# Strassen products of a feed-forward block in float32: copies that free PSUM banks put right behind their products, weight sums one split ahead, another order of small products

## The chip, the core and the metric

The kernel runs on one core of a Trainium2 chip. Its time is the device time of one execution in microseconds (us); the time before is the median of three runs. The engines are TensorE (PE, matrix products; PEld is its weight load), VectorE (DVE), ScalarE (ACT), GpSimd (POOL) and SyncE (SP), which here only issues DMAs. Each engine works through its own queue in order.

## The reference, cut to what matters

One step of a two-layer encoder for a prompt of 1024 frames and a sample of 32: in the first layer an mLSTM mixer, in the second a windowed attention, each followed by a SwiGLU feed-forward block. The change touches the feed-forward block alone:

```python
def swiglu(x, w_gu, w_down):
    g, u = jnp.split(x @ w_gu, 2, axis=-1)
    return (jax.nn.silu(g) * u) @ w_down
...
x = layer_norm(DEEPNORM_ALPHA * x + swiglu(x, w_gu[layer], w_down[layer]), ln_g[layer, 1], ln_b[layer, 1])
```

The model width is 1024, the inner width 2816, everything is float32.

## The kernel before, in words

**Float32 by three products.** Each operand is split into a high part (rounded to the PE's fp32r type) and the remainder. `gemm` (L404) issues three matmuls per tile of 128 rows: high by high (L412), high by low (L413), low by high (L414). Weights are split on the fly: ACT makes `wh` (L244), then POOL, for some units DVE, makes `wl` (L246).

**Seven products for eight.** The 1056 frames are four groups of 264 columns. In the feed-forward block a weight is halved both ways, a1, a2, b1, b2, and multiplied by Strassen's seven products in Winograd's form: a1, a2, b2 and the sums s1 to s4, with the operands x11, x21, x22 and t1 to t4 of the activations. Four DVE operations make the sums of a pair of raw weight tiles in place (L212 to L218). The inner width is 22 tiles of 128; tiles 2, 3, 20 and 21 of a layer are worked by `up_tile`, tiles 4 to 19 in eight *doubles* by `up_double(i)` (L1565), which takes tiles i and i + 1 as rows 0 and 1 and applies the seven-product scheme a second time to the products by a2: four small weights g1 to g4 (from the tile `wn`, with sums at L194 to L197) make seven small products into the PSUM tiles `chain` and `side`.

A large product is 24 matmuls of 264 columns, a small one 6. A double has 12 large and 7 small ones, 330 matmuls. `chain` accumulates, as bank A does: a1's product, then s2, s1 and s4 are added on top without clearing, and after each of the first three ACT copies the sum so far out of A (to gate0 at L1607, to up0 at L1618, to up1 at L1624); after s4 ACT applies SiLU (L1635). So the next product into A must wait for the copy. b2 and s3 go to bank B, of which a double has one; DVE adds them (L1621, L1627, L1628).

In a row the order of products is a1, the pair of small ones, s2, b2, s1, s3, (row 1: the pair for g3), s4 (row 1: g4).

**What sets the order of the other engines.** `Weights` keeps a list of split jobs. `_next` (L221) takes the next one: loads raw tiles if need be, makes the sums that this job needs on DVE (`_source`, L200, and `_inner`, L188), then issues ACT's copy and POOL's subtraction. `done` (L274) is called when a product has been issued and, with five slots, issues the split four jobs ahead. `mul` calls `done` at its end, and the copy out of A is issued after `mul`: behind that split in ACT's queue. The raw tiles (four buffers, `wr`) are loaded by `load_to` (L166) when a pair's last split, s4, has been issued, `wn` (one buffer) by `fetch` (L176) when g4's has.

**Staging.** `stage(p)` (L1375) is a task that runs beside the products: it takes finished inner tiles, makes t1 to t4 of them on DVE (L1398, L1399, L1404, L1411), splits each by `put` (ACT L1386, POOL or DVE L1387) and stores it (L1388, `hs`). It frees the buffer slots that later copies out of A write to. The down product reads the stores back.

## Time and profile before

| what | value |
|---|---|
| median of 3 runs | 2264.77 us (2258.8 to 2269.38) |
| the profiled execution | 2263.57 us, span 2261.8 us |
| mean granted PE clock | 0.994 |
| PE, PEld busy | 2185.3 us, 2147.7 us |
| DVE, ACT, POOL busy | 1567.8, 1015.0, 1077.7 us |
| the chain that ended last | PE 63%, DVE 15%, ACT 7% |

How to read the views: a group or timeline row names the line, the engine, the operation, what is written from what (128x512 is partitions by elements) and times. In a group row, behind the bar, stand busy time, mean ns of one, and the engine's idle time just before these instructions with what ended it. A timeline row has the start, the duration, and in brackets the idle time before it and the instruction that released it. A row of windows has the stretch, its length, then for PE, PEld, DVE, ACT and POOL busy time and count, the granted clock, the DMA engines' busy share and GB/s. A matmul's modelled duration is longer than the distance to the next one's start, because matmuls are pipelined.

### The profile page before, as it was taken

How to read it: one execution, taken by the hardware profiler on the slowest of the kernel's cores; microseconds unless marked ns; L12 is line 12 of the kernel's file. 1: busy time of each engine (PE TensorE's matmuls, PEld its weight loads, DVE VectorE, ACT ScalarE, POOL GpSimd, SP SyncE). 2: the span in 40 equal slices, each digit the busy share in tenths (PEclk: the TensorE clock that was granted, in tenths of full speed). 3: DMA queues.
4: the chain of work that ended last, by engine and by line, in shares of the span. 5: the costliest groups of instructions: out<-in, count | busy, mean ns of one | idle time of the engine just before them, and what ended most of it. 6: DMA issues, size and time to landing. Idle time of an engine off the chain costs nothing.

```text
span 2261.8 us, 44523 instructions
## 1 busy us (share of the span) xinstructions
PE 2185.3 (97%) x16990; PEld 2147.7 (95%) x16990; DVE 1567.8 (69%) x3008; ACT 1015.0 (45%) x2299; POOL 1077.7 (48%) x1014
## 2 busy tenths in 40 slices
PE   9999999999999999999999999999899999999997
PEld 9999999998899999999998999999899999999997
DVE  4465677787677776566667678888677777666657
ACT  4444455463444444422236778656344444431224
POOL 2544210004667667544526777501566766654431
PEclk9999999999999999999999999999999999999999
DMA  4222213113344444797515334412344344398622
GB/s 166 76 60 58 67 35 109 53 67 114 141 154 144 151 152 153 255 330 236 182 65 172 105 105 109 154 38 77 118 158 171 124 162 171 127 357 280 225 71 78
DMA packets 181414, 315.16 MB, mean 139 GB/s; under 512 B 18832, under 2 KB 131528, under 8 KB 181200
## 3 DMA queue, kind: packets, MB, share of 16 engines
q1 hardware_dynamic: 176848, 307.98, 41.2%
q10 hardware_dynamic: 4352, 4.33, 0.6%
q8 instruction: 134, 2.20, 0.4%
q14 instruction: 80, 0.66, 0.1%
HBM read 214.51 MB, written 87.27 MB: 133 GB/s over the span
## 4 chain that ended last, share of the span: by engine, by line
PE 63%; DVE 15%; ACT 7%; issue 6%; DMA 5%; POOL 4%; SPq 0%; POOLq 0%; ACTq 0%; DVEq 0%
PE d L412 9%; PE d L414 9%; PE d L413 9%; PE A L412 6%; PE A L414 6%; PE A L413 6%; PE B L412 4%; PE B L413 4%; PE B L414 4%; DMA wn<-in_gu 2%; DVE z L1599 1%; PE T L2021 1%; POOL wl_b L246 1%; DVE wr L218 1%; ACT act L515 1%
## 5 line engine op out<-in xcount | busy, mean ns | idle before, releaser
L246 POOL TENSOR_TENSOR wl_s<-wr,wh_s 128x512 fp32r<-128x512 f32 x224 | 329.1, 1488 | 203.6 <-ACT wh_s L244 152.2
L412 PE MATMUL d<-sx,wh 128*128 128x264 f32 (+2 forms) x1068 | 342.2, 320 | 2.5 <-ACT wh L244 2.4
L414 PE MATMUL d<-sx,wl 128*128 128x264 f32 (+2 forms) x1068 | 326.2, 305 | 2.7 <-POOL wl L246 2.7
L413 PE MATMUL d<-sx,wh 128*128 128x264 f32 (+2 forms) x1068 | 325.8, 305 | 0.2
L246 POOL TENSOR_TENSOR wl_a<-wr,wh_a 128x512 fp32r<-128x512 f32 x80 | 109.6, 1370 | 428.2 <-ACT wh_a L244 426.5
L412 PE MATMUL A<-sx,wh_s 128*128 128x264 f32 x896 | 259.2, 289 | 19.3 <-ACT z L1624 5.4
L244 ACT CAST wh_s<-wr 128x512 fp32r<-128x512 f32 x224 | 135.7, 618 | 284.6 <-DVE wr L216 256.6
L414 PE MATMUL A<-sx,wl_s 128*128 128x264 f32 x896 | 255.5, 285 | 0.0
L413 PE MATMUL A<-sx,wh_s 128*128 128x264 f32 x896 | 255.4, 285 | 0.0
L412 PEld LDWEIGHTS d<-sx,wh 128*128 128x128 f32 x1068 | 202.4, 189 | 6.1 <-ACT wh L244 3.1
L414 PEld LDWEIGHTS d<-sx,wl 128*128 128x128 f32 x1068 | 202.1, 189 | 3.9 <-POOL wl L246 3.6
L413 PEld LDWEIGHTS d<-sx,wh 128*128 128x128 f32 x1068 | 202.6, 190 | 1.6 <-DVE sx L443 0.8
L412 PEld LDWEIGHTS A<-sx,wh_s 128*128 128x128 f32 x896 | 169.9, 190 | 26.0 <-ACT z L1624 7.5
L412 PE MATMUL d<-sx,ex 128*128 128x264 f32 x624 | 180.5, 289 | 0.1
L413 PE MATMUL d<-sx,ex 128*128 128x264 f32 x624 | 177.2, 284 | 0.0
L414 PE MATMUL d<-sx,ex 128*128 128x264 f32 x624 | 176.9, 284 | 0.0
L414 PEld LDWEIGHTS A<-sx,wl_s 128*128 128x128 f32 x896 | 170.1, 190 | 0.0
L413 PEld LDWEIGHTS A<-sx,wh_s 128*128 128x128 f32 x896 | 170.0, 190 | 0.0
L412 PE MATMUL A<-ex,wh_s 128*128 128x264 f32 x448 | 130.1, 290 | 22.9 <-ACT z L1607 14.7
L246 POOL TENSOR_TENSOR wl<-wr,wh 128x512 fp32r<-128x512 f32 (+2 forms) x81 | 104.4, 1297 | 95.8 <-ACT wh L244 93.9
L2001 POOL TENSOR_SCALAR s<-s,st 128x256 f32<-128x256 f32 (+1 forms) x144 | 122.7, 864 | 44.6 <-DVE st L1999 29.9
L246 POOL TENSOR_TENSOR wl_g<-wn,wh_g 128x512 fp32r<-128x512 f32 x64 | 92.9, 1452 | 80.4 <-ACT wh_g L244 78.9
(438 smaller groups left out, 7464.6 us busy)
## 6 DMA issues: line engine op xcount, KB each, us to landing
wr<-in_gu SPq DMA_DIRECT2D x92, 512.0 KB, 5.1
hs_t<-act SPq DMA_DIRECT2D x64, 528.0 KB, 4.9
hs_x<-act SPq DMA_DIRECT2D x56, 528.0 KB, 2.9
sx<-hs_x SPq DMA_DIRECT2D x112, 264.0 KB, 6.0
sx<-hs_t SPq DMA_DIRECT2D x64, 264.0 KB, 6.0
ex<-hs_t SPq DMA_DIRECT2D x64, 264.0 KB, 6.3
wr<-in_dn SPq DMA_DIRECT2D x32, 512.0 KB
hs_x<-z SPq DMA_DIRECT2D x16, 528.0 KB, 6.2
```

The costliest lines, as they stand in the source:

```text
L218: sub(a2, a2, b2)
L244: self.nc.scalar.copy(hi, r)
L246: eng.tensor_sub(lo, r, hi.bitcast(F32))
L412: nc.tensor.matmul(out, ah, bh, start=start and k == 0, stop=False, **kw)
L413: nc.tensor.matmul(out, ah, bl, start=False, stop=False, **kw)
L414: nc.tensor.matmul(out, al, bh, start=False, stop=stop and k == last, **kw)
L515: nc.scalar.activation(z, z, AF.Identity, scale=gk, bias=bk)
L1599: nc.vector.tensor_mul(gate0[r], gate0[r], up0[r])
L2001: nc.gpsimd.tensor_scalar_mul(p[:R, h, lo:256], p[:R, h, lo:256], st[:R, 2, h : h + 1])
L2021: nc.tensor.transpose(pt[:nk, i, h, :R], p[:R, h, c : c + nk], ident[:R, :R])
```

## The change

It does five things: in `up_double`, the copies out of bank A (and the SiLU) are issued by a callback at the end of the product, before `done` issues the next split; the order of products in a row becomes a1, b2, s2, small pair, s1, s3 and the rest as before, with the job list to match; the four sums of a pair are formed in another order and in other places (s2 in a1's, s3 in b2's, s4 in a2's, s1 in b1's), and `prepare` issues those of the next job right behind the current split; loads of raw tiles and the fetch of `wn` are issued at the next job instead of at once; and the splits of the nested operands start 1.0 us later each.

```diff
-                self.jobs += [(u, f) for f in ("a1", "g1", "b2", "s2", "s1", "s3", "s4")]
-                self.jobs += [(v, "a1"), (u, "g2")] + [(v, f) for f in ("b2", "s2", "s1", "s3")]
-                self.jobs += [(u, "g3"), (v, "s4"), (u, "g4")]
+                self.jobs += [(u, f) for f in ("a1", "b2", "s2", "g1", "s1", "s3", "s4")]
+                self.jobs += [(v, f) for f in ("a1", "b2", "s2")] + [(u, "g2")]
+                self.jobs += [(v, f) for f in ("s1", "s3")] + [(u, "g3"), (v, "s4"), (u, "g4")]
...
-        if f == "g2":
-            s3, a1, a2, b1, b2 = (part(i) for i in range(5))
-            self.nc.vector.tensor_sub(s3, a1, b1)
-            self.nc.vector.tensor_add(b1, b1, b2)
-            self.nc.vector.tensor_sub(a1, b1, a1)
-            self.nc.vector.tensor_sub(a2, a2, a1)
...
+        self.prepare(u, f)
+        a, b = self.raw[u], self.raw[u + 1]
+        return {
+            "a1": a[:, :n], "a2": a[:, n : 2 * n], "b2": b[:, n : 2 * n],
+            "s1": b[:, :n], "s2": a[:, :n], "s3": b[:, n : 2 * n], "s4": a[:, n : 2 * n],
+        }[f]
+
+    def prepare(self, u, f):
+
+        if (u, f) in self.made or f not in ("s2", "s3", "s4", "g2"):
+            return
+        self.made.add((u, f))
         sub, add = self.nc.vector.tensor_sub, self.nc.vector.tensor_add
-        if f == "b2":
-
-            sub(a1, a1, b1)
-        elif f == "s2":
-
+        if f == "g2":
+            t = self.inner[u]
+            s3, a1, a2, b1, b2 = (t[:, 256 * i : 256 * (i + 1)] for i in range(5))
+            sub(s3, a1, b1)
+        else:
+            n = self.units[u].shape[-1] // 2
+            a, b = self.raw[u], self.raw[u + 1]
+            a1, a2, b1, b2 = a[:, :n], a[:, n : 2 * n], b[:, :n], b[:, n : 2 * n]
+        if f in ("s2", "g2"):
             add(b1, b1, b2)
+            sub(a1, b1, a1)
+        if f == "s3":
             sub(b2, b2, a1)
-        elif f == "s1":
-            sub(a2, a2, b2)
+        if f in ("s4", "g2"):
+            sub(a2, a2, a1)
...
+        self.load_to(self.due)
         self.load_to(u if f in (0, 1) else u + 1)
+        if self.owed:
+            self.owed = False
+            self.fetch()
...
         if f == "g4":
             del self.inner[u]
-            if self.nfetch % len(DOUBLES):
-                self.fetch()
-        if f in (1, "s4"):
+            self.owed = self.nfetch % len(DOUBLES) > 0
+        if f == 1:
             del self.raw[u]
-            if f == "s4":
-                del self.raw[u + 1]
-                u += 1
             self.load_to(u + self.depth)
+        if f == "s4":
+            del self.raw[u], self.raw[u + 1]
+            self.due = u + 1 + self.depth
+        if self.njob < len(self.jobs):
+            u, f = self.jobs[self.njob]
+            if u in self.inner if f == "g2" else u in self.raw and u + 1 in self.raw:
+                self.prepare(u, f)
...
                 hi, lo = nested[o]
-                yield 1.2
+                yield 2.2
...
-            def mul(row, ps, f, o, **kw):
+            def mul(row, ps, f, o, then=None, **kw):
...
+                if then:
+                    then()
                 W.done(us[row], f)
...
+            def copy_to(at, name, row, ps):
+                at[row] = take(row, name)
+                nc.scalar.copy(at[row], ps)
+
             for row in range(2):
                 a = bank("A")
-                mul(row, a, "a1", "x11")
-                gate0[row] = take(row, "g0")
-                nc.scalar.copy(gate0[row], a)
+                mul(row, a, "a1", "x11", lambda: copy_to(gate0, "g0", row, a))
                 finish_tile()
+                if not row:
+                    staging.append(wv.launch(stage(i // 2 - 1)))
+                b = bank("B")
+                mul(row, b, "b2", "t4")
+                mul(row, a, "s2", "t2", lambda: copy_to(up0, "u0", row, a), again=True)
+                nc.vector.tensor_add(up0[row], up0[row], b)
                 if row:
                     small(chain, "g2", 1, "t2", [(1, 0)], True, False)
                     small(side, "g2", 0, "t3", [(1, 1)])
                 else:
-                    staging.append(wv.launch(stage(i // 2 - 1)))
                     small(chain, "g1", 0, "x11", [(0, 0)], False, False)
                     small(side, "g1", 1, "x21", [(0, 0)])
-                mul(row, a, "s2", "t2", again=True)
-                up0[row] = take(row, "u0")
-                nc.scalar.copy(up0[row], a)
-                b = bank("B")
-                mul(row, b, "b2", "t4")
-                nc.vector.tensor_add(up0[row], up0[row], b)
-                mul(row, a, "s1", "t1", again=True)
-                up1[row] = take(row, "u1")
-                nc.scalar.copy(up1[row], a)
+                mul(row, a, "s1", "t1", lambda: copy_to(up1, "u1", row, a), again=True)
...
-                mul(row, a, "s4", "x22", again=True)
+                mul(row, a, "s4", "x22", lambda: nc.scalar.activation(take(row, "s1"), a, AF.Silu), again=True)
...
-                nc.scalar.activation(take(row, "s1"), a, AF.Silu)
```

Line numbers of the changed kernel are up to 18 higher. What moves on the engines is shown at three places, all at the seam between the fourth and the fifth double of the first layer.

ACT's queue before, from the split of the next double's g1 to the copy of up0. `wh_` names a split by its weight (a, b, s, g), `wr` and `wn` are raw weights, `A` the bank; L1386 is a staging cast, L1597 the SiLU of the double before, L1607 and L1618 are the copies to gate0 and up0.

```order
L244 CAST wh_g_8884<-wn_8833 128x512
L244 CAST wh_b_8914<-wr_8549 128x512
L244 CAST wh_s_8926<-wr_8549 128x512
L1635 ACTIVATE act<-A_8685 128x528
L1386 CAST act<-act 128x528
L1597 ACTIVATE z_4632<-z_4632 128x528 x2
L244 CAST wh_s_8968<-wr_8549 128x512
L1607 COPY act<-A_8934 128x528
L244 CAST wh_s_8988<-wr_8547 128x512
L1386 CAST act<-z_4632 128x528
L244 CAST wh_s_9020<-wr_8547 128x512
L1618 COPY z_4632<-A_8934 128x528
```

The same stretch of the change (all copies are L1624 now, the SiLU of s4 is L1650, staging L1403):

```order
L258 CAST wh_b_8885<-wr_8576 128x512
L1650 ACTIVATE act<-A_8684 128x528
L258 CAST wh_s_8916<-wr_8574 128x512
L258 CAST wh_g_8927<-wn_8862 128x512
L1403 CAST act<-act 128x528
L1616 ACTIVATE z_4632<-z_4632 128x528 x2
L1624 COPY act<-A_8933 128x528
L258 CAST wh_s_8967<-wr_8576 128x512
L258 CAST wh_s_8999<-wr_8576 128x512
L1403 CAST act<-z_4632 128x528
L1624 COPY z_4632<-A_8933 128x528
```

The SiLU of s4 has moved ahead of the split of s2, g1's split from ahead of b2's to behind s2's, and the split ahead of gate0's copy to behind it.

POOL's queue at the same place before, the low parts of the splits and the staging subtraction L1387:

```order
L246 TENSOR_TENSOR wl_a_8866<-wr_8547,wh_a_8865 128x512
L246 TENSOR_TENSOR wl_g_8885<-wn_8833,wh_g_8884 128x512
L246 TENSOR_TENSOR wl_b_8915<-wr_8549,wh_b_8914 128x512
L246 TENSOR_TENSOR wl_s_8927<-wr_8549,wh_s_8926 128x512
L1387 TENSOR_TENSOR act<-act 128x528
```

And in the change, where L1404 is the staging subtraction:

```order
L260 TENSOR_TENSOR wl_a_8866<-wr_8574,wh_a_8865 128x512
L260 TENSOR_TENSOR wl_b_8886<-wr_8576,wh_b_8885 128x512
L260 TENSOR_TENSOR wl_s_8917<-wr_8574,wh_s_8916 128x512
L260 TENSOR_TENSOR wl_g_8928<-wn_8862,wh_g_8927 128x512
L1404 TENSOR_TENSOR act<-act 128x528
```

g1's subtraction now stands directly ahead of the staging one, behind s2's.

SP's queue of DMAs before, at the fetch of `wn`; `hs_t` and `hs_x` are staging stores:

```order
L172 DMA wr_8800<-in_gu 128x1024
L172 DMA wr_8802<-in_gu 128x1024
L185 DMA wn_8833<-in_gu 128x512 x2
L1388 DMA hs_t_81<-act 128x1056
L1388 DMA hs_x_84<-act 128x1056
```

And in the change:

```order
L173 DMA wr_8826<-in_gu 128x1024
L173 DMA wr_8828<-in_gu 128x1024
L1405 DMA hs_t_81<-act 128x1056
L186 DMA wn_8862<-in_gu 128x512 x2
L1405 DMA hs_x_84<-act 128x1056
```

The fetch has moved behind one staging store.

8 lines of the change are left out of this document (3 added, 5 removed).

## The prediction, made before the change was run

> **What bounds the kernel now.** I read the page first: busy shares, then the groups, for where TensorE (PE) stands still.
>
> ```profile
> PE 2185.3 (97%) x16990; PEld 2147.7 (95%) x16990; DVE 1567.8 (69%) x3008; ACT 1015.0 (45%) x2299; POOL 1077.7 (48%) x1014
> L412 PE MATMUL A<-sx,wh_s 128*128 128x264 f32 x896 | 259.2, 289 | 19.3 <-ACT z L1624 5.4 <-ACT z L1470 4.5 <-ACT act L1477 4.1
> L412 PE MATMUL A<-ex,wh_s 128*128 128x264 f32 x448 | 130.1, 290 | 22.9 <-ACT z L1607 14.7 <-ACT act L1607 7.9
> ```
>
> TensorE bounds the kernel, and nothing in the change removes a product: all that can be won is time in which it stands still. The largest such groups are matmuls into bank A that wait for ScalarE (ACT) copies out of that bank (L1607, L1618 and L1624 in `up_double`, L1470 and L1477 in `up_tile`). A matmul's busy time is longer than its pitch, so idle time understates the loss. I count by stretches instead: time, and PE matmuls in brackets.
>
> ```profile
> 527.30:576.30 49.00, 42.07 (x326) 41.17 (x324) 30.98 (x35) 19.23 (x37) 24.28 (x19) 0.97 0.31 110
> 576.30:620.80 44.50, 40.91 (x330) 40.28 (x330) 30.75 (x37) 18.61 (x36) 30.82 (x22) 1.00 0.44 158
> 620.80:878.10 257.30, 245.31 (x1980) 241.54 (x1980) 188.62 (x217) 106.87 (x198) 178.25 (x121) 1.00 0.43 151
> 900.00:955.00 55.00, 55.00 (x455) 55.00 (x454) 27.27 (x33) 20.83 (x37) 30.20 (x23) 1.00 0.67 232
> 1581.50:1629.80 48.30, 41.92 (x325) 41.08 (x324) 31.02 (x35) 19.12 (x36) 24.22 (x19) 0.96 0.31 111
> 1629.80:1674.00 44.20, 42.14 (x330) 41.72 (x330) 31.58 (x37) 18.46 (x36) 30.36 (x22) 0.96 0.43 158
> 1674.00:1930.50 256.50, 245.57 (x1980) 241.80 (x1980) 193.62 (x217) 106.96 (x199) 178.78 (x121) 1.00 0.43 151
> ```
>
> The fourth row has no wait: 55.00/455 = 0.121 us a matmul, so 2.92 us for a product of 24 (by the row-to-row distances) and 0.73 for a small one of 6. The other rows exceed that pitch by 49.0 - 39.4 = 9.6, 44.5 - 39.9 = 4.6, 257.3 - 239.6 = 17.7, 9.0, 4.3 and 16.9: **62 us in all**, 2.7% of the span, and the ceiling of the change. A steady double (six in each long row) loses 17.7/6 to 16.9/6, say 2.9 us. Seven such periods in each layer are 41; the other 21 are lost in the two plain tiles ahead and the first double ("the front").
>
> Now one steady double, engine by engine, from the timeline. TensorE's rows (start, duration; in brackets the idle time before, and what ended it):
>
> ```profile
> 742.71 0.28 PE L412 MATMUL chain<-sx,wh_g 128*128 128x264 f32 x1
> 749.25 0.39 PE L412 MATMUL A<-ex,wh_s 128*128 128x264 f32 x1 [1.25 <-ACT act L1607]
> 752.28 0.28 PE L412 MATMUL B<-ex,wh_b 128*128 128x264 f32 x1
> 755.65 0.39 PE L412 MATMUL A<-sx,wh_s 128*128 128x264 f32 x1 [0.30 <-ACT z L1618]
> 762.01 0.39 PE L412 MATMUL A<-sx,wh_s 128*128 128x264 f32 x1 [0.26 <-ACT act L1624]
> ```
>
> I set t = 0 at 742.71, where s4 of the double before has ended and g4 (0.73) and a1 (2.92) follow; a1 ends at t = 3.65 (746.36). The two g1 products cover 1.46, so s2 could start at 747.82 and starts at 749.25: 1.4 late. What ACT did meanwhile:
>
> ```profile
> 744.81 0.62 ACT L244 CAST wh_s<-wr 128x512 fp32r<-128x512 f32 x1 [3.61 <-DVE wr L216]
> 745.34 0.61 ACT L1635 ACTIVATE act<-A 128x528 f32<-128x528 f32 x1
> 747.44 0.61 ACT L244 CAST wh_s<-wr 128x512 fp32r<-128x512 f32 x1
> 748.60 0.60 ACT L1607 COPY act<-A 128x528 f32<-128x528 f32 x1 [0.55 <-POOL act L1387]
> 753.94 0.63 ACT L1386 CAST act<-z 128x528 fp32r<-128x528 f32 x1 [4.23 <-DVE z L1399]
> 755.00 0.59 ACT L1618 COPY z<-A 128x528 f32<-128x528 f32 x1
> 760.84 0.62 ACT L244 CAST wh_g<-wn 128x512 fp32r<-128x512 f32 x1 [4.19 <-DVE wn L196]
> 772.61 0.60 ACT L1618 COPY z<-A 128x528 f32<-128x528 f32 x1 [2.28 <-PE A L414]
> ```
>
> ACT is not busy, it is blocked in order: a split stands ahead of the SiLU and waits 3.61 for VectorE's sum (L216); everything behind shifts; the copy then waits for GpSimd (L1387), which still reads the slot it writes. The later copies sit behind a staging cast and behind g2's split. The last row is a copy with a free road: 0.60 long. Its product ended when the next began, at 772.36:
>
> ```profile
> 772.36 0.28 PE L412 MATMUL B<-ex,wh_b 128*128 128x264 f32 x1
> ```
>
> so 0.25 passes before it, and 748.60 + 0.60 to 749.25 leaves 0.05 after it. **A copy needs 0.9 us of cover.**
>
> **The change part by part.** No engine gets an instruction more: four sums a pair before and after, the same copies, splits, loads. Only places move.
>
> *New order of products.* Between a1 and s2 stands b2 (2.92) instead of the pair g1 or g2 (1.46); between s2 and s1 now the pair. Covers of 2.92, 1.46 and 2.92 (row 1: 4.38) all exceed 0.9, if ACT is free. *Copies ahead of the split* and *sums one split ahead* are to make it free. DVE and POOL decide whether they do:
>
> ```profile
> 744.03 0.69 DVE L216 TENSOR_TENSOR wr<-wr,wr 128x512 f32<-128x512 f32 x1 [1.19 <-POOL wl_b L246]
> 745.98 1.40 DVE L1592 TENSOR_TENSOR act<-act,z 128x528 f32<-128x528 f32 x1 [0.91 <-ACT act L1635]
> 747.29 1.84 DVE L1599 TENSOR_TENSOR z<-z,act 128x528 f32<-128x528 f32 x1
> 750.77 1.78 DVE L218 TENSOR_TENSOR wr<-wr,wr 128x512 f32<-128x512 f32 x1
> 753.20 0.71 DVE L1399 TENSOR_TENSOR z<-z 128x528 f32<-128x528 f32 x1
> 746.76 1.80 POOL L1387 TENSOR_TENSOR act<-act 128x528 fp32r<-128x528 f32 x1
> 748.53 3.47 POOL L246 TENSOR_TENSOR wl_s<-wr,wh_s 128x512 fp32r<-128x512 f32 x2
> 777.63 0.80 SPq L185 DMA_DIRECT2D wn<-in_gu  x2
> 780.31 0.33 SPq L1388 DMA_DIRECT2D hs_t<-act  x1
> 783.38 0.62 ACT L244 CAST wh_g<-wn 128x512 fp32r<-128x512 f32 x1 [3.32 <-DMA wn<-in_gu]
> 784.08 1.73 POOL L246 TENSOR_TENSOR wl_g<-wn,wh_g 128x512 fp32r<-128x512 f32 x1 [2.65 <-ACT wh_g L244]
> 788.56 1.30 POOL L246 TENSOR_TENSOR wl_s<-wr,wh_s 128x512 fp32r<-128x512 f32 x1 [1.51 <-ACT wh_s L244]
> ```
>
> I walk the changed order by hand with these durations. ACT starts queued work about 0.52 apart (744.81, 745.34).
> - ACT: SiLU at 0.25 (was 2.63); s2's split 0.75, its sums being ready (L216 needed b2's split on POOL first; the new sum reads parts split long before); g1's split when the wn fetch has landed. That fetch now stands behind an hs store and its split behind s2's. It took 5.75 from issue to use (777.63 to 783.38). The store went at 780.31; its cast now stands behind one more split (0.52), and its own issue takes 0.33, so the fetch goes at 781.16 and lands at 786.9. The next double starts a period of 42.8 after 742.71, at 785.5: t = 1.4. Split 1.45, staging cast 2.0, SiLUs 2.5 and 3.1.
> - POOL: wl_s 1.45 to 2.75, wl_g (1.73) to 4.48, staging L1387 (1.80) to 6.28. That one still reads the slot that gate's copy writes, so the copy runs 6.33 to 6.93. s2 could start at 0.73 + 2.92 + 2.92 = 6.57 and starts at 6.98: **0.4 lost** (now 1.4).
> - DVE: behind the first SiLU (3.15) the two of L1599 (1.84 each), the sum for s3 (1.78), two staging sums (0.71 each): 10.03. The staging cast that waits for the last (L1399) starts then, the copy of up0 runs 10.55 to 11.15; s2 ends at 9.90, the pair at 11.36. s1 is in time by 0.15, but only while the staging sums meet an idle POOL; I allow **0.2 lost** for a part of them that doesn't (now 0.5, with 2.92 of cover).
> - Copy of up1: g2's split no longer stands ahead of it; s3 covers it. Row 1: nothing ahead of its three copies waits; as now, 0.
>
> With 0.1 for a restart (s2 from 749.25 to 752.28 is 3.03, not 2.92), 0.7 per double instead of 2.9. Ends of this term: 0 (each slip is below half a microsecond) and 2.7 (0.4 + 0.1, and s1 2.0 late, as under the rivals); I take the walked 0.7, so 16 x 0.7 = 11 stay.
>
> Here a rule weighs against the change. The rows: L216 took 0.69 with POOL idle, L218 1.78 beside POOL's 3.47, L1399 0.71 after it. The Trainium skill, "GPSIMD Engine Reference", section "8. Key points", says that GpSimd shares its SBUF interfaces with VectorE and contends with instructions that have two SBUF inputs; the trace agrees (0.69 against 1.78). By that rule a fuller POOL stretches the staging sums, which is the second rival below; without it no sum could be stretched and 16 x 0.2 = 3 us more be won.
>
> *The front.* Its copies were late behind nested casts and g1's split, which waits for wn. The second is moved off (the first fetch comes later, and its split stands behind s1's copy), of the first one cast fewer stands ahead. Ends: all 21 stay, or none; I take a third, 7, as one of its two kinds of wait goes by order alone and the other shortens. Part of the front is the clock:
>
> ```profile
> 565.86 0.39 PE L412 MATMUL A<-sx,wh_s 128*128 128x264 f32 x1 [3.09 <-ACT act L1477]
> 566.00:568.00 2.00, 2.00 (x11) 2.00 (x12) 0.04 (x1) 0.85 (x2) 2.00 (x3) 0.57 0.00 0
> ```
>
> After the wait of 3.09 the granted clock is 0.57, and the rows at 0.97, 0.96 and 0.96 above hold 1.5 + 1.9 + 1.8 = 5 us of it; steady doubles, with waits near 1.25, show 1.00. The Trainium skill, "TensorE: Matmul & The Clock Gate", section "Part 1: The HAM clock gate (the "warmup" mystery)", says that the clock is halved after an idle window of about 3.4 us; by it these stretches go with the waits, as in my third; were they unrelated, 5 us less would be won.
>
> *Loads later.* Each raw load goes one split (2.92) later; its pair is used some 20 us after it (seven products), so 17 stay against the 5.75 that the fetch took: 0, and nothing to gain, as no copy waits for a raw load. In the down stage only sums and loads move, and the fourth window row, plain tiles and the stage's start without a wait, is the cover: 0. If that cover went, a late load would show as a wait of ACT's splits.
>
> **Sum:** 62 - 11 - 7 = 44 us. The profiled execution took 2263.57 (span 2261.8, 1.8 around it): 2219.6. The median shown is 1.2 higher: **2221**.
>
> **The rivals.**
> - *GpSimd holds the slot longer.* For: the copy already waits 0.55 for L1387, and two subtractions now stand ahead of it, not one. Against: b2 covers 1.46 more. One us later: 1.7 a double, 62 - 27 - 7 = 28, **2237**.
> - *The wait moves to s1.* Both staging sums meet POOL and take 1.8 instead of 0.7: up0's copy 2.2 later, s1 2.0 late, 2.5 a double; 62 - 40 - 7 = 15, **2250**. For: POOL's two splits (3.47) come right behind the slot's reader now as before. Against: DVE's chain starts 2.4 earlier, as the SiLU does (0.25 for 2.63).
> - *Nothing comes of it:* the second rival with the front unmended, 62 - 40 - 21 = 1: **2264**.
> - *Slower: the fetch.* g1's split stands ahead of gate's copy, and the fetch behind a staging store on SP's queue.
>
> ```profile
> SPq L1388 <- POOL act L1387: 434.9, 68, 10.9
> ```
>
>   Such stores held SP 434.9/68 = 6.4 us on average. The walk has 0.7 to spare (the split must end before wl_s does, at 2.75). With 6.4 more, each double loses 0.7 + 5.7 = 6.4, 3.5 above now: 56 more, less the front's 14: **2307**. It turns slower once the fetch is some 3.8 late (0.7 + 2.2, and 14/16 for the front). Against: the store ahead of it (t-series) waits for DVE, not POOL.
>
> **How the numbers follow.** Forecast 0.67, GpSimd 0.15, s1 0.10, nothing 0.04, fetch 0.04. The forecast's own range is 2203 (all 62 won) to 2230 (1.3 a double); with GpSimd's the range 2203 to 2240 leaves out 0.18. A measurement of this kernel tells about 0.5% (11 us) from no change: faster 0.92, same 0.04, slower 0.04.
>
> **What would show it.** Right: steady doubles of 40 to 41 us instead of 42.8; no SiLU behind a waiting split; waits of s2 for the gate's copy below 0.5 us; no row-0 wait of s4; granted clock 1.00 in the front; ACT's wait for VectorE's weight sums (L216) gone. Wrong: ACT waiting for wn ahead of the gate's copy, s1 waiting 1 us or more on up0's copy, or matmuls into B waiting for VectorE.

## The result, and the profile after

| kernel | median, us | range, us | ratio to before (95% interval) |
|---|---|---|---|
| before, measured beside it | 2262.28 | 2258.8 to 2269.38 | 1 |
| changed | 2239.31 | 2238.36 to 2239.95 | 0.9894 [0.9868, 0.9921] |

The change makes the kernel faster by 1.1%: 23 us, where 44 were forecast. The time lies 0.7 us inside the upper end of the range (2203 to 2240) and outside the forecast's own (2203 to 2230). The profiled execution took 2239.93 us (span 2238.1), 23.6 less than that of before.

The page of the changed kernel; L429 to L431 are the three matmuls of `gemm`, all copies out of bank A are now L1624:

```profile
PE 2177.6 (97%) x16990; PEld 2142.6 (96%) x16990; DVE 1570.8 (70%) x3008; ACT 1024.1 (46%) x2299; POOL 1076.4 (48%) x1014
L429 PE MATMUL A<-sx,wh_s 128*128 128x264 f32 x896 | 255.0, 285 | 3.2 <-ACT act L1624 2.2
L429 PE MATMUL A<-ex,wh_s 128*128 128x264 f32 x448 | 129.0, 288 | 5.8 <-ACT z L1624 3.1
```

No engine has an instruction more or less (PE's busy time falls by 7.7 us all the same: a matmul's duration is modelled, and longer behind a wait). What fell is the idle time ahead of the matmuls by s weights: 19.3 us is 3.2 now, 22.9 is 5.8. Next the stretches of the changed kernel by the same method, each row from a product's start to a product's start. For each layer there are four: the plain tiles ahead of the doubles, the first double, six steady doubles, and the first seven weight pairs of the down stage:

```profile
527.00:568.80 41.80, 41.27 (x338) 40.91 (x337) 34.17 (x35) 18.37 (x33) 25.39 (x18) 1.00 0.37 128
568.80:612.70 43.90, 40.81 (x332) 40.21 (x330) 31.77 (x39) 18.46 (x34) 30.10 (x21) 1.00 0.44 160
612.70:860.47 247.77, 243.72 (x1980) 241.38 (x1980) 193.38 (x217) 110.15 (x200) 176.16 (x120) 1.00 0.45 156
935.80:1088.18 152.38, 145.94 (x1178) 144.50 (x1177) 96.03 (x143) 32.86 (x56) 66.44 (x51) 0.99 0.81 270
1569.20:1611.10 41.90, 41.37 (x338) 40.99 (x337) 34.48 (x35) 18.39 (x33) 25.75 (x18) 1.00 0.36 128
1611.10:1654.50 43.40, 40.78 (x332) 40.18 (x330) 29.65 (x38) 18.44 (x34) 29.33 (x21) 1.00 0.44 161
1654.50:1902.90 248.40, 243.54 (x1980) 241.19 (x1980) 193.89 (x218) 109.96 (x200) 176.71 (x120) 1.00 0.44 156
1978.06:2128.11 150.05, 144.30 (x1178) 142.86 (x1177) 96.04 (x143) 32.86 (x56) 66.43 (x51) 1.00 0.82 272
```

And the same seven pairs before:

```profile
955.24:1099.88 144.64, 143.12 (x1179) 142.75 (x1177) 97.21 (x141) 31.68 (x54) 68.67 (x51) 1.00 0.84 279
2007.48:2151.68 144.20, 143.01 (x1178) 142.76 (x1177) 97.20 (x141) 31.68 (x54) 68.63 (x51) 1.00 0.84 279
```

At 0.121 us a matmul the feed-forward rows lose 0.9, 4.0, 8.2, 1.0, 3.5 and 8.8: 26 us, where before lost 62. So 36 us were won there. The down stage gives back 152.38 - 144.64 = 7.7 and 150.05 - 144.20 = 5.9, together 14. 36 - 14 = 22 is the measured gain; the trace accounts for all but a microsecond. The rows of the two plain tiles ahead of the doubles are clean: 0.9 and 1.0 lost where it was 9.6 and 9.0, at a granted clock of 1.00 where it was 0.97 and 0.96. The first double of each layer has gained little: 4.0 and 3.5 lost where it was 4.6 and 4.3.

TensorE's waits of the changed kernel name the culprits (engine, bank and line that waits, what it waited for, us in total, times, the longest):

```profile
PE A L429 <- ACT wh_s L258: 11.2, 14, 2.0
PE A L429 <- ACT act L1624: 4.5, 6, 1.8
PE B L429 <- DVE z L1646: 4.3, 5, 1.9
```

The first row is the down stage, and new: 14 waits, one for each of the seven pairs of two layers. It names ScalarE's split. The third is new as well, in the doubles: matmuls into bank B that wait for VectorE.

**The down stage, closer.** VectorE, then TensorE, around the start of a pair in the changed kernel:

```profile
977.04 2.77 DVE L1768 TENSOR_TENSOR act<-act,B 128x528 f32<-128x528 f32 x4 [0.75 <-PE B L431]
979.73 0.68 DVE L224 TENSOR_TENSOR wr<-wr 128x512 f32<-128x512 f32 x1
980.50 0.69 DVE L225 TENSOR_TENSOR wr<-wr,wr 128x512 f32<-128x512 f32 x1
981.11 1.31 DVE L1766 SCALAR_TENSOR_TENSOR act<-act,A 128x528 f32<-128x528 f32 x2
981.91 0.36 PE L429 MATMUL A<-ex,wh_a 128*128 128x264 f32 x1 [0.56 <-ACT wh_s L258]
```

And before:

```profile
993.75 2.77 DVE L1751 TENSOR_TENSOR act<-act,B 128x528 f32<-128x528 f32 x4 [0.74 <-PE B L414]
996.43 0.68 DVE L212 TENSOR_TENSOR wr<-wr,wr 128x512 f32<-128x512 f32 x1
997.03 0.70 DVE L1749 SCALAR_TENSOR_TENSOR act<-act,A 128x528 f32<-128x528 f32 x1
997.89 0.31 PE L412 MATMUL A<-ex,wh_a 128*128 128x264 f32 x1
```

The adds of s4 (L1766, before L1749) free the bank that the next pair's a1 writes. Between s3's four adds and them stood one weight sum, L212; now there are two, L224 and L225, since `prepare` makes s2's sums right behind the split of b2. The first of the two L1766 ends near 981.11 + 0.70, and TensorE starts at 981.91. ScalarE's split, which the label names, ended about then too. So there are two theories for these 14 waits, and the trace alone doesn't part them.

**The doubles, closer.** GpSimd, ScalarE and TensorE at row 0's s2 of the changed kernel; then VectorE and TensorE at row 1's b2 of the double before, 25 us earlier:

```profile
816.79 1.78 POOL L1404 TENSOR_TENSOR act<-z,act 128x528 fp32r<-128x528 f32 x1
818.61 0.60 ACT L1624 COPY z<-A 128x528 f32<-128x528 f32 x1 [3.13 <-POOL act L1404]
819.26 0.39 PE L429 MATMUL A<-ex,wh_s 128*128 128x264 f32 x1 [0.58 <-ACT z L1624]
```

```profile
789.16 0.42 DVE L218 TENSOR_TENSOR wn<-wn 128x256 f32<-128x256 f32 x1
790.08 1.47 DVE L225 TENSOR_TENSOR wn<-wn 128x256 f32<-128x256 f32 x1
793.57 0.69 DVE L1646 TENSOR_TENSOR z<-z,B 128x528 f32<-128x528 f32 x1
794.41 0.36 PE L429 MATMUL B<-ex,wh_b 128*128 128x264 f32 x1 [0.61 <-DVE z L1646]
```

The first is the forecast's own 0.4, gate's copy behind GpSimd's slot: 0.58. The second was not forecast: in the new order row 1's b2 comes two products behind row 0's s3, bank B exists once, and the adds that empty it (L1645, L1646) stand behind the four sums of wn, which `prepare` now issues ahead of them. Two of these sums run beside GpSimd's subtractions and take 1.47 and 1.45 us where the others take 0.42.

### The profile page after: what moved, and what is told of

The parts are those of the page before. It is cut to its first block, busy times and chain, and to the rows that moved or that the text cites. A ratio compares the mean times of both kernels' runs of the same rounds, so it can differ in the third digit from the quotient of the medians.

```text
span 2238.1 us, 44402 instructions
## 1 busy us (share of the span) xinstructions
PE 2177.6 (97%) x16990; PEld 2142.6 (96%) x16990; DVE 1570.8 (70%) x3008; ACT 1024.1 (46%) x2299; POOL 1076.4 (48%) x1014
## 5 line engine op out<-in xcount | busy, mean ns | idle before, releaser
L429 PE MATMUL d<-sx,wh 128*128 128x264 f32 (+2 forms) x1068 | 341.9, 320 | 3.2 <-ACT wh L258 2.8
L431 PE MATMUL d<-sx,wl 128*128 128x264 f32 (+2 forms) x1068 | 326.3, 305 | 2.8 <-POOL wl L260 2.7
L429 PE MATMUL A<-sx,wh_s 128*128 128x264 f32 x896 | 255.0, 285 | 3.2 <-ACT act L1624 2.2
L431 PE MATMUL A<-sx,wl_s 128*128 128x264 f32 x896 | 254.2, 284 | 0.0
L430 PE MATMUL A<-sx,wh_s 128*128 128x264 f32 x896 | 254.2, 284 | 0.0
L429 PEld LDWEIGHTS d<-sx,wh 128*128 128x128 f32 x1068 | 202.4, 190 | 6.7 <-ACT wh L258 3.4
L431 PEld LDWEIGHTS d<-sx,wl 128*128 128x128 f32 x1068 | 202.0, 189 | 4.0 <-POOL wl L260 3.7
L429 PE MATMUL d<-sx,ex 128*128 128x264 f32 x624 | 180.5, 289 | 0.1
L431 PE MATMUL d<-sx,ex 128*128 128x264 f32 x624 | 176.9, 284 | 0.0
L429 PEld LDWEIGHTS A<-sx,wh_s 128*128 128x128 f32 x896 | 168.6, 188 | 4.4 <-ACT act L1624 2.7
L431 PEld LDWEIGHTS A<-sx,wl_s 128*128 128x128 f32 x896 | 168.7, 188 | 0.0
L429 PE MATMUL A<-ex,wh_s 128*128 128x264 f32 x448 | 129.0, 288 | 5.8 <-ACT z L1624 3.1
L430 PE MATMUL A<-ex,wh_s 128*128 128x264 f32 x448 | 127.2, 284 | 0.0
```

The costliest lines, as they stand in the source:

```text
L429: nc.tensor.matmul(out, ah, bh, start=start and k == 0, stop=False, **kw)
L430: nc.tensor.matmul(out, ah, bl, start=False, stop=False, **kw)
L431: nc.tensor.matmul(out, al, bh, start=False, stop=stop and k == last, **kw)
```

## The experiments

All are made from the changed kernel, but for two that are made from the kernel before; each was timed beside the kernel before.

| edit | median, us | ratio to before (95% interval) |
|---|---|---|
| down stage's sums for s2 late | 2226.05 | 0.9837 [0.9823, 0.9850] |
| loads at once | 2239.09 | 0.9895 [0.9882, 0.9909] |
| s3's adds first | 2227.50 | 0.9846 [0.9832, 0.9859] |
| g1's low part on VectorE | 2232.54 | 0.9872 [0.9857, 0.9886] |
| both: down sums late, adds first | 2213.65 | 0.9784 [0.9770, 0.9797] |
| copies and SiLU behind the split | 2227.21 | 0.9849 [0.9836, 0.9863] |
| old order of products | 2294.82 | 1.0145 [1.0131, 1.0159] |
| no sums ahead | 2225.91 | 0.9841 [0.9828, 0.9854] |
| SiLU alone behind the split | 2229.77 | 0.9854 [0.9838, 0.9871] |
| before, with the new order alone | 2227.74 | 0.9845 [0.9830, 0.9860] |
| both, and only up0's copy ahead | 2205.31 | 0.9747 [0.9733, 0.9762] |
| before, with copies and SiLU ahead alone | 2287.16 | 1.0120 [1.0101, 1.0138] |

The next table shows where seven of the kernels lose time, in us and in both layers together, each stretch from a product's start to a product's start and counted at 0.121 us a matmul as above. The plain tiles end here where the first double begins, while the rows above run on to its first s2. The pitch without waits is a hair above 0.121, which adds up to 3 us to the column of the doubles.

| kernel | two plain tiles ahead | eight doubles | two plain tiles behind | seven down pairs |
|---|---|---|---|---|
| before | 14.4 | 49.5 | 0.2 | 4.2 |
| changed | 0.8 | 26.7 | 0.3 | 17.9 |
| copies and SiLU behind the split | 0.8 | 17.4 | 0.3 | 16.4 |
| no sums ahead | 10.2 | 17.9 | 3.2 | 2.8 |
| before, with the new order alone | 4.4 | 25.2 | 0.3 | 4.6 |
| before, with copies and SiLU ahead alone | 13.9 | 72.2 | 1.0 | 3.9 |
| both, and only up0's copy ahead | 0.8 | 8.7 | 0.3 | 2.6 |

### The down stage: its sums, or its loads?

The new set `later` holds the weight pairs of the down stage.

```diff
-            if u in self.inner if f == "g2" else u in self.raw and u + 1 in self.raw:
+            if f == "s2" and u in self.later:
+                pass
+            elif u in self.inner if f == "g2" else u in self.raw and u + 1 in self.raw:
                 self.prepare(u, f)
```

> The changed kernel, with one edit: in the down stage the two sums for s2 are no longer made one split ahead, but with s2's own split. Theory (VectorE's queue): the 14 waits that the trace names after ScalarE's split wh_s (0.56 us each, 1.96 at the first pair of a layer) are in truth waits for VectorE's adds L1766, which free bank A and stand behind these two sums (0.68 + 0.69 us). They vanish but for the first of each layer; the stage takes 7.7 us (layer 0) and 5.9 us (layer 1) less, the kernel about 2226 us where the changed kernel takes 2239.3. Rival (the split itself, or the later loads, hold TensorE): the sums now come later still, so the splits do too; the waits stay or grow, 2239 us or more.

Measured: 2226.05 us, 13.3 less than the changed kernel. VectorE and TensorE at the start of the same pair (the adds are L1771 and L1769 here):

```profile
973.76 2.77 DVE L1771 TENSOR_TENSOR act<-act,B 128x528 f32<-128x528 f32 x4 [0.75 <-PE B L434]
976.66 0.70 DVE L1769 SCALAR_TENSOR_TENSOR act<-act,A 128x528 f32<-128x528 f32 x1
977.90 0.28 PE L432 MATMUL A<-ex,wh_a 128*128 128x264 f32 x1
```

No sum stands between the adds, and a1 starts without a wait. The waits for wh_s are gone from the list, though the split itself now comes later; only the first pair of each layer still waits for the adds, 0.57 and 0.59 us. So VectorE's queue was the cause, and the label was the wrong one of two things that ended together.

```diff
-            self.due = u + 1 + self.depth
+            self.load_to(u + 1 + self.depth)
...
-            self.owed = self.nfetch % len(DOUBLES) > 0
+            if self.nfetch % len(DOUBLES):
+                self.fetch()
```

> The changed kernel, with the raw loads and the fetch of wn issued at once again, as before the change. Theory (queues of VectorE and GpSimd): the later loads cost nothing in the down stage and win nothing in the doubles; 2239 us, within 2 us. Rival (the later loads make the 14 waits of the down stage): those waits vanish, 2226 us. Second rival (the fetch ahead of a staging store is what the later fetch avoided): the doubles lose up to 1 us each, 2250 us or more.

Measured: 2239.09 us, and the 14 waits stay (10.9 us). The later loads and the later fetch are worth nothing in either direction.

### The doubles: the adds out of bank B, and GpSimd's load

```diff
+                def spread():
+                    nc.vector.tensor_add(up0[row], up0[row], b)
+                    nc.vector.tensor_add(up1[row], up1[row], b)
+
-                mul(row, b, "s3", "t3")
-                nc.vector.tensor_add(up0[row], up0[row], b)
-                nc.vector.tensor_add(up1[row], up1[row], b)
+                mul(row, b, "s3", "t3", spread)
```

> The changed kernel, with the two adds of s3's product out of bank B (L1645, L1646) issued by a callback ahead of the next split, so ahead of the four sums of wn in VectorE's queue. Theory (row 1's b2 waits for these adds, for they stand behind the sums): the waits of matmuls into B on VectorE in the doubles vanish (five on z L1646 with 4.3 us, and one on act L1646), with restarts about 6 us: 2233 us. Rival (which wait a double has is a matter of its phase, and the wait for the gate's copy takes the other's place, about 0.57 us a double): 2237 to 2239 us, with more waits of matmuls into A on copies.

Measured: 2227.50 us, 11.8 less. No matmul into B waits for a double's adds any more; the waits of row 0's s2 stay. The mechanism is right, its size was taken too small: two more waits into B (1.4 us), which the trace of the changed kernel put down to ScalarE's copy, went as well. The list misses part of it too: counted from product to product, row 1's b2 came 0.3 us or more late in 14 of the 16 doubles of the changed kernel, 10 us in all, and in six of the 14 the idle time shown is 0.10 us or less. Here it is on time everywhere.

```diff
+    on_vector.update((u, "g1") for u in doubles)
```

> The changed kernel, with the low part of g1 made by VectorE and not by GpSimd (1.73 us off GpSimd ahead of the staging subtraction whose slot the gate's copy writes). Theory (row 0's s2 waits for the gate's copy, and that for GpSimd): the copy's wait for L1404 ends 1.7 us earlier and the waits of s2 in the doubles (12, 7 us with restarts) vanish but for the front: 2234 us, if VectorE takes the 0.7 to 1.8 us without a new wait. Rival (VectorE is the next bound): the waits for L1646 in row 1 take their place, 2239 us or more.

Measured: 2232.54 us, 6.8 less, near the theory's 2234; but its trace shows that both theories had a part. Row 0's s2 waits only once any more, for 0.14 us, so GpSimd's load ahead of the slot's reader did hold the gate's copy. In some doubles s1 now waits 0.4 to 1.1 us for up0's copy, and waits of b2 for s3's second add stay. The wait went down the row rather than away.

```diff
+            if f == "s2" and u in self.later:
...
+                mul(row, b, "s3", "t3", spread)
```

> The changed kernel with both edits that won: the two adds of s3's product ahead of the next split (that alone gave 2227.5 us), and the down stage's sums for s2 with their own split (that alone gave 2226.05). Theory (the two waits lie in different stages, so the gains add): 2239.3 - 11.8 - 13.3, 2214 us. Rival (one of them moves the other's wait elsewhere): 2220 us or more.

Measured: 2213.65 us. The two gains add, so they are separate waits in separate stages.

### Which part won?

```diff
                     gemm(ps[:, c, :], w, tiles(X[o](c)), **kw)
+                W.done(us[row], f)
                 if then:
                     then()
-                W.done(us[row], f)
```

> The changed kernel, with the copies out of bank A and the SiLU issued behind the next split again, as before the change. New order and sums ahead stay. Theory (a copy behind a split whose sums are ready starts 0.5 us later, behind one that waits for the sums of wn up to 2 us): the SiLU of s4 stands behind g2's split and is late, up0's copy has 1.46 us of cover; about 0.5 to 1.5 us a double more, 2247 to 2262 us. Rival (order and sums ahead have done it all): 2239 to 2243 us.

Measured: 2227.21 us, *faster* by 12.1. Both theories of mine were wrong: the part that the change is named after costs time where it stands. That called for another theory, tested below. In its trace row 0's s2 waits nowhere, and row 1's b2 only in the two first doubles (0.44 and 0.59 us), though the adds still stand behind the sums of wn. At the place of the rows above, the adds out of B end 22.6 us after the last g4's start (790.08 - 767.49) and not 23.6 (794.26 - 770.70), since a weight sum ahead of them (L224) takes 0.68 us and not 1.77. So this gain and that of s3's adds first are in part the same waits. In exchange s1 waits 0.35 to 0.40 us for up0's copy in each steady double.

```diff
-                self.jobs += [(u, f) for f in ("a1", "b2", "s2", "g1", "s1", "s3", "s4")]
-                self.jobs += [(v, f) for f in ("a1", "b2", "s2")] + [(u, "g2")]
+                self.jobs += [(u, f) for f in ("a1", "g1", "b2", "s2", "s1", "s3", "s4")]
+                self.jobs += [(v, "a1"), (u, "g2"), (v, "b2"), (v, "s2")]
...
-                yield 2.2
+                yield 1.2
...
-                b = bank("B")
-                mul(row, b, "b2", "t4")
-                mul(row, a, "s2", "t2", lambda: copy_to(up0, "u0", row, a), again=True)
-                nc.vector.tensor_add(up0[row], up0[row], b)
                 if row:
...
                     small(side, "g1", 1, "x21", [(0, 0)])
+                mul(row, a, "s2", "t2", lambda: copy_to(up0, "u0", row, a), again=True)
+                b = bank("B")
+                mul(row, b, "b2", "t4")
+                nc.vector.tensor_add(up0[row], up0[row], b)
```

> The changed kernel, with the products of a double, and the list of splits, in the order before the change (a1, small pair, s2, b2, s1, s3), and with the nested operands' splits at their old times, which that order needs. Copies ahead of the split and sums ahead stay. Theory (b2 behind a1 gives the gate's copy 2.92 us of cover where the pair gives 1.46): s2 waits 1.4 to 2 us for the gate's copy in each double, 22 to 32 us more; row 1's b2 comes later behind s3, and its waits for L1646 (about 6 us) vanish; about 2257 us. Rival (the order is of no weight): 2239 us; if it only costs the waits for L1646: 2233 us.

Measured: 2294.82 us, 55.5 more than the changed kernel and 33 more than before. The direction was right, the price too low. TensorE's largest wait in this kernel:

```profile
PE A L429 <- ACT z L1624: 19.0, 10, 2.7
```

With the waits on the copies to `act` (12.0 us, 6 times) s2 waits 1.9 us a double on average, and counted from product to product it loses 33 us more than in the changed kernel, about as forecast. Nobody had forecast the rest: matmuls into B wait 17.0 us for the add of b2's product (L1641), 24 us from product to product. The new order is the part that wins, and without it the others together lose.

```diff
+            self.prepare(u, f)
             return self._inner(u, f)
...
-        if self.njob < len(self.jobs):
-            u, f = self.jobs[self.njob]
-            if u in self.inner if f == "g2" else u in self.raw and u + 1 in self.raw:
-                self.prepare(u, f)
```

> The changed kernel, with no sums made ahead anywhere: each split's sums are issued with it, as before the change, in the new form. Order and copies ahead of the split stay. Theory (sums ahead win in the doubles, as ScalarE's splits no longer wait, and cost in the down stage): the down stage gives back its 14 waits (13 us), the doubles lose about 1 us each to copies behind waiting splits; about 2241 us. Rival (with the copies ahead of the split the sums ahead win nothing): 2226 us, as with the down stage's sums alone, or less, since the sums of wn then come behind L1646 too.

Measured: 2225.91 us, the rival's number, but by luck: three parts add up to it (table by stage above). The down stage loses 15 us less. The doubles lose 9 less, for row 1's b2 waits no more. And the plain tiles lose 12 more: there TensorE waits 7.4 us (4 times, up to 2.6) for a copy of `up_tile` (L1484), which stands behind a split that waits for its sums (2.69 us for VectorE's L230 at the first such place). So sums ahead win in the plain tiles, and cost in the doubles and in the down stage.

### Why copies ahead of the split cost time

In the changed kernel, at the end of a double (TensorE's g4, whose start is t = 0; then the SiLU of s4, the split of the next double's s2, GpSimd's part of that, the staging subtraction, and the gate's copy that waits for it):

```profile
770.70 0.28 PE L429 MATMUL chain<-sx,wh_g 128*128 128x264 f32 x1
770.90 0.61 ACT L1650 ACTIVATE z<-A 128x528 f32<-128x528 f32 x1 [3.83 <-PE A L431]
771.41 0.61 ACT L258 CAST wh_s<-wr 128x512 fp32r<-128x512 f32 x1
772.10 1.74 POOL L260 TENSOR_TENSOR wl_s<-wr,wh_s 128x512 fp32r<-128x512 f32 x1 [3.34 <-ACT wh_s L258]
775.05 1.78 POOL L1404 TENSOR_TENSOR act<-act 128x528 fp32r<-128x528 f32 x1
776.87 0.60 ACT L1624 COPY act<-A 128x528 f32<-128x528 f32 x1 [2.10 <-POOL act L1404]
```

ScalarE stands for 3.83 us until s4 has ended, GpSimd for 3.34 behind it. The split behind the SiLU needs nothing of s4; its sums are ready. Theory: the SiLU ahead of it holds it up. The next kernel moves the SiLU alone:

```diff
-                if then:
+                if then and f in ("a1", "s2", "s1"):
                     then()
                 W.done(us[row], f)
+                if then and f not in ("a1", "s2", "s1"):
+                    then()
```

> The changed kernel, with the SiLU of s4 alone issued behind the next split again; the three copies out of bank A stay ahead. All copies behind gave 2227.2 us. Theory (with its sums made ahead, the split of the next double's s2 could run before s4 ends; the SiLU ahead of it, which must wait for s4's end, holds it up, with it GpSimd's subtractions and the slot that the gate's copy needs): nearly all of that gain comes from the SiLU, 2227 to 2230 us, and row 0's waits for the gate's copy go. Rival (one of the copies, by the same holding up in ScalarE's queue, does it): 2239 us, or part of the way, 2234 to 2237.

Measured: 2229.77 us, 9.5 of the 12.1. The same place (g4 starts first; the SiLU is L1652, the copy L1626):

```profile
766.53 0.28 PE L429 MATMUL chain<-sx,wh_g 128*128 128x264 f32 x1
766.00 0.62 ACT L258 CAST wh_s<-wr 128x512 fp32r<-128x512 f32 x1 [3.11 <-DVE wr L225]
766.79 0.61 ACT L1652 ACTIVATE z<-A 128x528 f32<-128x528 f32 x1 [0.17 <-PE A L431]
766.70 1.30 POOL L260 TENSOR_TENSOR wl_s<-wr,wh_s 128x512 fp32r<-128x512 f32 x1 [2.12 <-PE A L431]
770.07 1.79 POOL L1404 TENSOR_TENSOR act<-act 128x528 fp32r<-128x528 f32 x1
771.89 0.60 ACT L1626 COPY act<-A 128x528 f32<-128x528 f32 x1 [1.54 <-POOL act L1404]
```

The split runs 0.53 before g4's start; in the changed kernel it ran 0.71 behind it (771.41 - 770.70). The gate's copy comes at 5.36 and not at 6.17, and in the steady doubles three matmuls into A still wait, none longer than 0.32 us. The SiLU loses 0.06 us by it. The Trainium skill, "PSUM — Partial Sum Buffer", section "Engine vs sequencer instructions", says that the queues of ScalarE, VectorE and GpSimd are strictly first in, first out; the trace agrees: one instruction that waited 3.83 us held a ready one for 1.2.

The same theory must hold without the rest of the change. So the callbacks alone, in the kernel before:

```diff
-                mul(row, a, "a1", "x11")
-                gate0[row] = take(row, "g0")
-                nc.scalar.copy(gate0[row], a)
+                mul(row, a, "a1", "x11", lambda: copy_to(gate0, "g0", row, a))
...
-                mul(row, a, "s2", "t2", again=True)
-                up0[row] = take(row, "u0")
-                nc.scalar.copy(up0[row], a)
+                mul(row, a, "s2", "t2", lambda: copy_to(up0, "u0", row, a), again=True)
...
-                mul(row, a, "s1", "t1", again=True)
-                up1[row] = take(row, "u1")
-                nc.scalar.copy(up1[row], a)
+                mul(row, a, "s1", "t1", lambda: copy_to(up1, "u1", row, a), again=True)
...
-                mul(row, a, "s4", "x22", again=True)
+                mul(row, a, "s4", "x22", lambda: nc.scalar.activation(take(row, "s1"), a, AF.Silu), again=True)
...
-                nc.scalar.activation(take(row, "s1"), a, AF.Silu)
```

> The kernel before, with the callbacks alone: the three copies out of bank A and the SiLU of s4 of a double issued ahead of the next split. Old order, sums with their split, loads at once. Theory (the SiLU ahead holds up a split that could run earlier): here it is the split of b2 that has to wait for the end of s4; GpSimd's part of it, VectorE's sum for s2 (which waits for that), s2's split and the staging subtraction behind it all come 1 to 2 us later, and so does the gate's copy; s2 waits 2 to 3 us for it where it waited 1.25, less 0.6 a double won at the copies of up0 and up1: 2270 to 2290 us. Rival (copies ahead win what they were forecast to win, the waits for up0's and up1's copies and part of that for the gate's): 2245 to 2255 us.

Measured: 2287.16 us, *slower* than before by 1.2%. In this kernel (g4's start, SiLU, b2's split, the sum for s2, the staging subtraction, the gate's copy at L1607, s2):

```profile
702.53 0.28 PE L412 MATMUL chain<-sx,wh_g 128*128 128x264 f32 x1
702.73 0.61 ACT L1632 ACTIVATE act<-A 128x528 f32<-128x528 f32 x1 [2.50 <-PE A L414]
703.24 0.61 ACT L244 CAST wh_b<-wr 128x512 fp32r<-128x512 f32 x1
705.25 0.69 DVE L216 TENSOR_TENSOR wr<-wr,wr 128x512 f32<-128x512 f32 x1 [2.61 <-POOL wl_b L246]
708.02 1.76 POOL L1387 TENSOR_TENSOR act<-z,act 128x528 fp32r<-128x528 f32 x1
709.82 0.60 ACT L1607 COPY z<-A 128x528 f32<-128x528 f32 x1 [1.60 <-POOL act L1387]
710.47 0.59 PE L412 MATMUL A<-ex,wh_s 128*128 128x264 f32 x1 [2.33 <-ACT z L1607]
```

b2's split ran 2.12 ahead of g4 before, and 0.71 behind it here:

```profile
740.59 0.61 ACT L244 CAST wh_b<-wr 128x512 fp32r<-128x512 f32 x1
```

From t = 0 (742.71 before, 702.53 here) L216 comes at 2.72 and not 1.32, the staging subtraction at 5.49 and not 4.05, the gate's copy at 7.29 and not 5.89: each 1.4 late, and s2 waits 2.33 where it waited 1.25. Matmuls into B wait too, for L1623 (14 times, 0.55 each). What the rival claimed came as well: the waits for the copies of up0 and up1, 10.4 us in the kernel before, are all gone. Copies and SiLU were not parted in this kernel; the rows show the SiLU's part.

### The order alone, and the best version

Of the change, the kernel before gets only this:

```diff
-                self.jobs += [(u, f) for f in ("a1", "g1", "b2", "s2", "s1", "s3", "s4")]
+                self.jobs += [(u, f) for f in ("a1", "b2", "s2", "g1", "s1", "s3", "s4")]
...
-                yield 1.2
+                yield 2.2
...
+                b = bank("B")
+                mul(row, b, "b2", "t4")
+                mul(row, a, "s2", "t2", again=True)
...
```

> The kernel before, with the new order of the products of a double alone (the list of splits to match, and the nested operands' splits 1.0 us later each, which belongs to it). Copies behind the splits, sums with their split, loads at once. Theory (the order did it: leaving out copies ahead or sums ahead cost nothing): no waits in the down stage, doubles no worse than in the changed kernel, 2226 us or less. Rival (order needs one of the others: with both left out a copy stands behind a split that waits for its sums): part of the gain, 2240 to 2255 us.

Measured: 2227.74 us. The order alone wins 34.5 us, more than the whole change. By stage 24 of them lie in the doubles and 10 in the two plain tiles ahead, whose own products kept their order; what did it there, the list of splits or the later splits of the nested operands, was not told apart. What is left in the doubles is s1, which waits for up0's copy (L1615 here) behind a split, nearly 1 us a double:

```profile
PE A L412 <- ACT z L1615: 9.4, 10, 1.0
```

That is the one copy with short cover, and the one that should go ahead.

The last kernel has both edits that won, and of the callbacks only up0's copy and the adds of s3 ahead of the split:

```diff
+                if then and f in ("s2", "s3"):
                     then()
                 W.done(us[row], f)
+                if then and f not in ("s2", "s3"):
+                    then()
```

> The changed kernel with both edits that won (adds of s3 first, the down stage's sums for s2 late; 2213.65 us), and of the copies out of bank A only up0's (cover 1.46 us) ahead of the split; the copies of gate0 and up1 and the SiLU behind it. Theory (a copy with 2.92 us of cover loses nothing behind a ready split, and the split held up by the SiLU is what delays GpSimd): the waits that are left in the doubles (about 0.6 us a double) go, 2205 to 2209 us. Rival (the gains overlap, as adds first had already taken these waits): 2212 us or more.

Measured: 2205.31 us, 0.9747 of before: 1.5% better than the change. Its steady doubles:

```profile
609.75:850.63 240.88, 240.69 (x1979) 240.34 (x1978) 188.36 (x217) 111.53 (x199) 175.65 (x121) 1.00 0.46 160
```

240.88 - 239.6 = 1.3 us in six doubles: 0.2 each, where before lost 2.9 and the change 1.4.

## Why the prediction was right in sign and wrong by half

- **The ceiling and the method held.** 62 us of TensorE's standing time; the best version takes the steady doubles to 0.2 each, and its total gain of 57 us is within it. A slip of 1 us: 0.7 was taken off 16 doubles, while the 62 holds 14 steady periods.
- **New order: right, and the largest part.** Covers of 2.92, 1.46 and 2.92 were the argument, "if ACT is free"; the order alone wins 34.5 us, though up0's copy, behind a split, then keeps s1 waiting nearly 1 us, and undoing it (with the nested splits' old times) costs 55.5.
- **The walk of GpSimd's queue was right to 0.2 us, in part by luck.** Split at 0.71 for 0.75, GpSimd's part at 1.40 for 1.45, the staging subtraction at 4.35 for 4.48, the gate's copy at 6.17 for 6.33. But g1's part took 1.29 where 1.73 was put in, s2's 1.74 for 1.30, and on VectorE the sum for s3 0.68 for 1.78, the last staging sum 1.68 for 0.71; these errors cancel. At this place s2 loses 0.4 in all, where 0.4 and 0.1 for a restart were forecast; in 9 of the 14 steady periods it waits 0.46 to 0.58 and then restarts, so that the average is 0.7 a double.
- **The step that failed: "In the down stage only sums and loads move [...] is the cover: 0."** It measured 14 us (some 1.5 of them by a slower clock, told below). The named cover was TensorE's lack of waits, not a look at the queue that the sums go into. On VectorE two sums of 0.68 came ahead of the adds that free bank A, and one had already been all that fitted: before, the first add ended at 997.73 and a1 began at 997.89. I named ScalarE's splits as the sign to look for; the trace even showed that sign, and it was the wrong one.
- **A second: "Row 1: nothing ahead of its three copies waits; as now, 0."** The copies indeed don't wait, but b2 does: on VectorE's adds out of bank B, behind the sums of wn. I had listed the symptom ("matmuls into B waiting for VectorE") as what would be wrong, and not priced it. With s2's 0.7 and 0.6 here, the doubles keep 1.4 where 0.7 was forecast: 9 us.
- **A step that was taken with the wrong sign: "Copies ahead of the split [...] are to make it free."** The walk put the SiLU at 0.25 instead of 2.63 and counted that as help. Nobody on TensorE waits for the SiLU soon, while the split behind it is on the path to the gate's copy. This costs 9.5 us in the changed kernel, 12 with the copies; in the kernel before, copies and SiLU ahead cost 25.6, while the copies of up0 and up1 did win their waits there.
- **The front: the number was right, the reason in part.** 7 of 21 were forecast to stay. The rows above lose 26 us; 14 steady periods of 1.4 are 20 of them, and 6 to 7 stay in the front. It runs at a clock of 1.00; the longest wait there is 1.90 us. What the forecast gave as reasons, one nested cast fewer and g1's split moved off, is not all: without sums ahead the plain tiles lose 10 us again, so these had a part there that the forecast didn't name.
- **The rivals.** The fetch (slower) is out: loads and fetch at once give the same time. The GpSimd rival has the nearest time (2237), but only part of its mechanism came, waits of up to 0.58 for 0.4 and not one of 1.4. The range reached 2240 for that rival alone, so that 2239.31 lies inside it is luck. The wait at s1 shows in the first double of each layer (1.84 and 0.41 us); otherwise it came only when g1's low part left GpSimd, or when up0's copy stood behind a split.

Not tried: sums ahead alone in the kernel before. The kernel with copies behind differs from the order alone by the sums ahead, in their new form, and by the later loads, which were worth nothing. It loses 8 us less in the doubles, s1's wait being 0.4 and not 0.95, 4 less in the plain tiles, and 12 more in the down stage. So sums ahead have some worth, and lose it again where the adds behind them come late.

## What to carry to other kernels

Before an instruction is moved ahead in an engine's queue, ask what it waits for: put ahead of a ready one, it lends that one its wait, and the cost shows on a third engine. Sums made early are free only as long as the adds that empty an accumulator, and stand behind them, still come in time, so look at the queue into which work is moved, in every stage that shares the code. And price each part by itself: here one of five parts won more than all five, and one of the others made the kernel slower alone.

## What was not expected of the hardware

- A wait that the profile gives as 0.56 us of TensorE cost 0.8: a pair of the down stage took 21.2 us (981.91 to 1003.12) instead of 20.4 (997.89 to 1018.33 before). The idle time counts from the modelled end of the last matmul, 0.28 us after its start, where the next one would have started 0.12 after it: 0.16 of the difference. The product behind a wait takes some 0.08 longer (2.98 us for 2.91).
- Two like waits left the clock unlike. The first pair of the down stage waits 1.96 us in the first layer and 1.97 in the second (at 2001.10). Behind the first the granted clock was 0.50:

```profile
959.22 0.36 PE L429 MATMUL A<-sx,wh_a 128*128 128x264 f32 x1 [1.96 <-ACT wh_s L258]
960.00:962.00 2.00, 2.00 (x11) 2.00 (x11) 0.21 (x1) 0.00 (x0) 1.76 (x2) 0.50 1.06 385
```

  That product took 4.52 us; behind the second wait the clock stayed at 1.00 and the product took 2.98. It is most of why the down stage gave back 7.7 us in one layer and 5.9 in the other. With loads at once both layers show the 0.50. The idle window of about 3.4 us of the Trainium skill, "TensorE: Matmul & The Clock Gate", section "Part 1: The HAM clock gate (the "warmup" mystery)", which the prediction quotes, is longer than these waits: here less was enough, though not always.
- The sums of wn, 128x256 elements, took 0.42 us each while GpSimd stood and 1.47 beside its subtractions: 3.5 times, and that helped to put L1646 late. The Trainium skill, "GPSIMD Engine Reference", section "8. Key points", says that GpSimd contends with VectorE instructions that have two SBUF inputs, and the trace agrees (1.47 against 0.42).
- A wait is put down to the last thing that ended by the profile. Twice here (ScalarE's wh_s in the down stage, its copy in the doubles) that was off by a hair, and only moving the other candidate told.
